# MLA's rotary scores: the two mixed products of a head as one matmul over both halves of the partitions

## The chip, the cores and the metric

The kernel runs on one core of one Trainium2 chip. The metric is device time in microseconds (us); the figure for a kernel is the median of several runs. All times below are in us unless marked otherwise. PE is the matrix engine (TensorE), DVE the vector engine, ACT the scalar engine, POOL GpSimd, and SP issues most of the transfers. PSUM is the memory that PE writes its results to; SBUF is the working memory that all engines read.

## The reference, cut to what matters

One encoder layer on 256 tokens of width 2048: a mixing block (MLA and differential attention side by side, one input projection, one output projection), cross-attention into 256 memory tokens, a SwiGLU feed-forward of 5632, and a final norm. All in float32. The change is in the MLA scores:

```python
s = (jnp.einsum('bqhd,bkhd->bhqk', qn_b, k_nope)      # 8 heads, d = 128
     + jnp.einsum('bqhr,bkr->bhqk', qr_b, k_rope))    # r = 64, one rotary key for all heads
p = jax.nn.softmax(s.astype(jnp.float32) * scale, axis=-1).astype(v.dtype)
```

`q_rope` has 64 numbers for each of 8 heads and passes through a rotation by position; `k_rope` has 64 numbers and is shared by all heads.

## The kernel before, in words

Each float32 operand of a matmul is held as a pair: a high part `h`, the value rounded to fp32r by ACT, and a low part `l`, the rest, subtracted by DVE (`split_into`, L99 and L100). `mm` (L91 to L93) then makes a product in three passes: h·h, h·l and l·h.

Each weight piece arrives in a raw tile (`wraw`, 3 buffers), is split into `wh` (ACT, L99) and `wl` (DVE, L100), 1024 numbers a partition at a time (4 buffers each), and is multiplied into an accumulator in PSUM (`acc`, pool `pacc`, 4 tiles). A second pool in PSUM, `pps`, has 4 tiles of 128x512 and serves everything else on the way: transposes (`pt`), the results of `stationary` (`qT`, `kT`), scores (`psc`), transposed probabilities (`ppt`), products with the values (`po`). A PSUM tile becomes free when its last reader on ACT or DVE is done.

The MLA part runs so. The latents are normalized and transposed into `cqT` and `ckvT` (the latter shares a tile, `lat`, with the rotary keys `krT`). A projection makes the rotary queries `qr`, which DVE rotates. Then for each group `hg` of four heads come queries `qT` and keys `kT` (`stationary`, PE passes of 256 columns) and values `vv` (`values`, an accumulator split into `val_h` and `val_l`). In the first group the rotary queries are transposed in between: 8 transposes into two `pt` tiles, each read by one ACT cast (`qrT_h`) and one DVE subtraction (`qrT_l`). Two heads share a 128-partition block of `qrT`, 64 partitions each; the keys `krT[:, 0]` and `krT[:, 1]` hold the 64 rotary numbers on the one or the other half with zeros on the rest, so that a matmul over 128 partitions picks one head.

The scores of a head and of 128 queries (`scores`) are six passes of 256 columns: three for the 128 plain dimensions and three for the rotary ones. The softmax is a chain over the engines: DVE takes the maximum (`nm`, L432) and scales it (L433), ACT takes the exponentials (`e`, L437), DVE the reciprocal (`rs`, L440) and the scaling (L459), PE transposes (`ppt`, L448), ACT and DVE split the result into `pT_h` and `pT_l`, and PE multiplies with the values (`po`).

What runs beside this on PE are the projections of differential attention (`acc<-wh,x0T`: 128x512, weights `in_w_in`), which need nothing from MLA but accumulators and the weight splits. The order on each engine is not written by hand: the tile framework's scheduler works it out when the program is built, from its own estimates, and it chooses which PSUM slot a new tile takes. On the chip each engine takes its instructions in that fixed order and waits on semaphores; an instruction that waits holds everything behind it on its engine.

## Time and profile before

| | |
|---|---|
| median of 3 runs | 1160.01 (1159.96 to 1160.74) |
| profiled execution | 1160.6, of which the span from first to last instruction is 1158.8 |
| granted PE clock, mean | 0.998 |
| PE busy | 1149.4 of 1158.8 |
| DVE busy | 900.3 |
| ACT busy | 612.1 |
| transfers | 222.13 MB, mean 192 GB/s |

A row of the timeline has the start of an instruction, how long it was busy, its engine, its source line, operation, and what it wrote from what; `x2` means that two equal ones are merged into a row. The busy times of successive instructions overlap a little, so the step from one start to the next (the pitch) is what a queue of them costs.

### The profile page before, as it was taken

The page shows a single profiled execution, that of the slowest core. Times are in us where ns is not written, and L with a number is a line of the kernel's source. Part 1 is how long each engine was busy: PE and PEld are TensorE (multiplying, and loading weights), DVE is VectorE, ACT ScalarE, POOL GpSimd, SP SyncE. Part 2 cuts the span into 40 slices and gives each one's busy share as a digit, 9 for nine tenths or more (in the row PEclk, how much of TensorE's full clock was granted, in tenths as well). Part 3 has the DMA queues.
Part 4 walks back from the last instruction along what each step waited for, and adds up shares of the span by engine and source line. Part 5 has one row for each costly group of instructions (what it writes and reads, how often), then busy time and mean ns, then how long its engine had stood idle before and what let it go on. Part 6 is the DMA issues. An engine that isn't in the chain of part 4 may idle for free.

```text
span 1158.8 us, 14403 instructions
## 1 busy us (share of the span) xinstructions
PE 1149.4 (99%) x5512; PEld 961.6 (83%) x5512; DVE 900.3 (78%) x1192; ACT 612.1 (53%) x866; POOL 69.8 (6%) x81
## 2 busy tenths in 40 slices
PE   9999999999999999999999999999999999999997
PEld 7888888888888888888888888888888888888887
DVE  7588766586867776978888787797888788798873
ACT  6755454554665565655444554564544554554552
POOL 4920000001000000000000000000000000000021
PEclk9999999999999999999999999999999999999999
DMA  9665334445754445465555555655556555565551
GB/s 349 222 205 189 125 137 166 170 146 201 279 210 182 145 147 185 177 218 183 184 213 185 205 185 191 218 180 184 200 186 217 205 181 203 188 220 207 211 198 73
DMA packets 33620, 222.13 MB, mean 192 GB/s; under 512 B 4112, under 2 KB 4752, under 8 KB 8848
## 3 DMA queue, kind: packets, MB, share of 16 engines
q1 hardware_dynamic: 32400, 217.29, 52.4%
q0 software_dynamic: 864, 3.15, 0.8%
q8 instruction: 43, 0.70, 0.2%
q10 hardware_dynamic: 288, 0.79, 0.2%
q14 instruction: 25, 0.20, 0.0%
HBM read 219.11 MB, written 2.10 MB: 191 GB/s over the span
## 4 chain that ended last, share of the span: by engine, by line
PE 98%; issue 0%; DMA 0%; DVE 0%; ACT 0%; SPq 0%; POOLq 0%; POOL 0%; DVEq 0%; ACTq 0%
PE acc L91 28%; PE acc L92 28%; PE acc L93 28%; PE q L91 2%; PE q L92 2%; PE q L93 2%; PE pt L301 2%; PE ppt L448 1%; PE psc L93 1%; PE psc L92 1%; PE psc L91 1%; PE acckv L91 0%; PE acckv L93 0%; PE acckv L92 0%; PE pt L824 0%
## 5 line engine op out<-in xcount | busy, mean ns | idle before, releaser
L99 ACT CAST wh<-wraw 128x1024 fp32r<-128x1024 f32 (+2 forms) x398 | 399.4, 1015 | 386.6 <-PE acc L93 344.4
L100 DVE TENSOR_TENSOR wl<-wraw,wh 128x1024 fp32r<-128x1024 f32 (+2 forms) x398 | 468.4, 1185 | 165.9 <-ACT wh L99 163.9
L92 PE MATMUL acc<-wl,x2n_h 128*128 128x512 f32 x480 | 185.5, 390 | 0.0
L93 PE MATMUL acc<-wh,x2n_l 128*128 128x512 f32 x480 | 185.3, 389 | 0.0
L91 PE MATMUL acc<-wh,x2n_h 128*128 128x512 f32 x480 | 160.5, 390 | 0.0
L93 PEld LDWEIGHTS acc<-wh,x2n_l 128*128 128x128 f32 x480 | 90.1, 188 | 19.0
L91 PEld LDWEIGHTS acc<-wh,x2n_h 128*128 128x128 f32 x480 | 90.1, 188 | 19.0 <-issue 0.2
L92 PEld LDWEIGHTS acc<-wl,x2n_h 128*128 128x128 f32 x480 | 90.1, 188 | 18.7
L92 PE MATMUL acc<-wl,hT_h 128*128 128x512 f32 (+1 forms) x272 | 103.7, 381 | 0.0
L93 PE MATMUL acc<-wh,hT_l 128*128 128x512 f32 (+1 forms) x272 | 103.5, 380 | 0.0
L91 PE MATMUL acc<-wh,hT_h 128*128 128x512 f32 (+1 forms) x272 | 89.4, 382 | 0.0
L92 PE MATMUL acc<-wl,x0T_h 128*128 128x512 f32 x224 | 88.2, 394 | 0.1
L93 PE MATMUL acc<-wh,x0T_l 128*128 128x512 f32 x224 | 87.9, 393 | 0.0
L91 PE MATMUL acc<-wh,x0T_h 128*128 128x512 f32 x224 | 87.7, 396 | 0.0
L99 ACT CAST wh<-tsum 128x1024 fp32r<-128x1024 f32 x56 | 58.3, 1048 | 42.5 <-DVE tsum L698 31.1
L100 DVE TENSOR_TENSOR wl<-tsum,wh 128x1024 fp32r<-128x1024 f32 x56 | 67.9, 1218 | 9.3 <-ACT wh L99 9.3
L91 PEld LDWEIGHTS acc<-wh,hT_h 128*128 128x128 f32 x272 | 51.2, 188 | 9.9 <-issue 0.2
L93 PEld LDWEIGHTS acc<-wh,hT_l 128*128 128x128 f32 x272 | 51.2, 188 | 9.6
L92 PEld LDWEIGHTS acc<-wl,hT_h 128*128 128x128 f32 x272 | 51.2, 188 | 9.5
L91 PEld LDWEIGHTS acc<-wh,x0T_h 128*128 128x128 f32 x224 | 42.3, 189 | 9.0 <-ACT wh L99 1.1
L92 PEld LDWEIGHTS acc<-wl,x0T_h 128*128 128x128 f32 x224 | 42.2, 188 | 8.3 <-DVE wl L100 0.8
L93 PEld LDWEIGHTS acc<-wh,x0T_l 128*128 128x128 f32 x224 | 42.2, 188 | 7.4
(361 smaller groups left out, 2008.4 us busy)
## 6 DMA issues: line engine op xcount, KB each, us to landing
wraw<-in_w_gu SPq DMA_DIRECT2D x80, 1024.0 KB, 4.8
wraw<-in_w_dn SPq DMA_DIRECT2D x36, 1024.0 KB, 4.8
wraw<-in_w_in SPq DMA_DIRECT2D x24, 1024.0 KB, 4.8
wraw<-in_w_out SPq DMA_DIRECT2D x16, 1024.0 KB, 4.9
wraw<-in_w_down SPq DMA_DIRECT2D x8, 1024.0 KB, 4.8
wraw<-in_w_in_lat SPq DMA_DIRECT2D x7, 832.0 KB, 7.2
wraw<-in_w_xk SPq DMA_DIRECT2D x4, 1024.0 KB, 5.8
wraw<-in_w_xq SPq DMA_DIRECT2D x4, 1024.0 KB, 4.8
```

What stands on the lines that cost most here:

```text
L91: nc.tensor.matmul(o, l.h, r.h, start=start, stop=False)
L92: nc.tensor.matmul(o, l.h, r.l, start=False, stop=False)
L93: nc.tensor.matmul(o, l.l, r.h, start=False, stop=stop)
L99: last_cast[0] = nc.scalar.copy(out=dst.h, in_=src).ins
L100: last_split[0] = nc.vector.tensor_tensor(out=dst.l, in0=src, in1=dst.h.bitcast(F32), op=ALU.subtract).ins
L301: nc.tensor.transpose(out=pt[:, j * P:(j + 1) * P], in_=src[:, j * P:(j + 1) * P], identity=ident)
L448: nc.tensor.transpose(out=pt[:, kt * S + tt * P:kt * S + (tt + 1) * P], in_=p[:, tt, kt * P:(kt + 1) * P], identity=ident)
```

## The change

`krT` and the rotary queries are laid out anew. `krT.h` stays. In the half of the partitions where `krT.h[:, o]` has the keys' high part, `krT.l[:, o]` now has a second copy of it, and in the other half the low part. The queries get three tiles instead of two: `qr_h` (the high parts, as before) and `qr_x0`, `qr_x1`, one for each parity of the head, with the low part of the own head on its half and the value again, rounded to fp32r, on the other half. One matmul of `qr_x[o]` with `krT.l[:, o]` then adds up l·h on one half of the partitions and h·l on the other, so a head and 128 queries take five passes instead of six.

```diff
+    def rope_keys(kr, tt):
+        pt = ps_tile("pt")
+        for j in range(2):
+            nc.tensor.transpose(out=pt[:, j * P:(j + 1) * P], in_=kr[:, j * P:(j + 1) * P], identity=ident)
+        pv = pt[:, :2 * P].rearrange("p (j t) -> p j t", t=P)
+        tok = slice(tt * P, (tt + 1) * P)
+        nc.scalar.copy(out=krT.h[:, :, tok], in_=pv)
+        for o in range(2):
+            own = slice(o * 64, o * 64 + 64)
+            nc.scalar.copy(out=krT.l[own, o, tok], in_=pv[own, o])
+            nc.vector.tensor_tensor(out=krT.l[own, 1 - o, tok], in0=pv[own, o],
+                                    in1=krT.h[own, o, tok].bitcast(F32), op=ALU.subtract)
...
-            transposed(krT, kr, tt, 2)
+            rope_keys(kr, tt)
...
-    qrT = act_tile(name="qrT")
+    qr_h = act.tile([P, 4, S], F32R, name="qr_h", tag="act")
+    qr_x = [act.tile([P, 4, S], F32R, name=f"qr_x{o}", tag="act") for o in range(2)]
...
+    def rope_queries(src, tt):
+        pt = ps_tile("pt")
+        for j in range(4):
+            nc.tensor.transpose(out=pt[:, j * P:(j + 1) * P], in_=src[:, j * P:(j + 1) * P], identity=ident)
+        pv = pt.rearrange("p (j t) -> p j t", t=P)
+        tok = slice(tt * P, (tt + 1) * P)
+        nc.scalar.copy(out=qr_h[:, :, tok], in_=pv)
+        for o in range(2):
+            own, other = slice(o * 64, o * 64 + 64), slice((1 - o) * 64, (1 - o) * 64 + 64)
+            nc.vector.tensor_tensor(out=qr_x[o][own, :, tok], in0=pv[own], in1=qr_h[own, :, tok].bitcast(F32),
+                                    op=ALU.subtract)
+            nc.scalar.copy(out=qr_x[o][other, :, tok], in_=pv[own])
...
-                transposed(qrT, qrs[tt], tt, 4)
+                rope_queries(qrs[tt], tt)
...
-    def scores(qs, ks):
+    def scores(q, k, rope=()):
...
-            for n, (q, k) in enumerate(zip(qs, ks)):
-                mm(ps[:, tt * S:(tt + 1) * S], q[:, tt * P:(tt + 1) * P], k, n == 0, n == len(qs) - 1)
+            mm(o, q[:, tok], k, True, not rope)
+            for n, (l, r) in enumerate(rope):
+                nc.tensor.matmul(o, l[:, tok], r, start=False, stop=n == len(rope) - 1)
...
-            ps = [scores([qT[hg][:, h, :], qrT[:, 2 * hg + hp, :]], [kT[hg][:, h, :], krT[:, h % 2, :]])
+            ps = [scores(qT[hg][:, h, :], kT[hg][:, h, :],
+                         [(qr_h[:, 2 * hg + hp, :], krT.h[:, h % 2, :]),
+                          (qr_x[h % 2][:, 2 * hg + hp, :], krT.l[:, h % 2, :])])
```

The other calls of `scores` only change their form. The scheduler lays the program out anew. From a point in the second projection of differential attention on, the rest of PE's, DVE's and ACT's lists is the same in both programs (4580 matmuls and transposes on PE), and POOL's and SP's lists are the same throughout. Between the rotary keys and that point three places differ most.

DVE, around the rotary queries, before (a row has line, operation, what it writes from what, and the engines or transfer queues whose semaphores it waits for):

```order
L100 TENSOR_TENSOR wl<-wraw,wh 128x1024 [waits DMAHW5_49,Activation_49]
L100 TENSOR_TENSOR qrT_l<-pt,qrT_h 128x4x128 [waits Activation_49] x2
L491 SCALAR_TENSOR_TENSOR neg_lam<-lexp 128x1 [waits Activation_49]
L100 TENSOR_TENSOR kT_l<-kT,kT_h 128x512 [waits Activation_49]
L100 TENSOR_TENSOR val_l<-acc,val_h 128x512 [waits Activation_49] x2
L100 TENSOR_TENSOR wl<-wraw,wh 128x1024 [waits DMAHW6_49,PE_49,Activation_49]
```

and in the changed program:

```order
L100 TENSOR_TENSOR wl<-wraw,wh 128x1024 [waits DMAHW5_49,Activation_49]
L437 TENSOR_TENSOR qr_x_770<-pt,qr_h 64x4x128 [waits Activation_49] x2
L526 SCALAR_TENSOR_TENSOR neg_lam<-lexp 128x1 [waits Activation_49]
L100 TENSOR_TENSOR wl<-wraw,wh 128x1024 [waits DMAHW6_49,PE_49,Activation_49]
L437 TENSOR_TENSOR qr_x_771<-pt,qr_h 64x4x128 [waits Activation_49] x2
L100 TENSOR_TENSOR kT_l<-kT,kT_h 128x512 [waits Activation_49] x2
```

The subtractions for `kT_l` have moved behind a weight split and behind two more subtractions.

ACT at the same place, before:

```order
L99 CAST qrT_h<-pt 128x4x128 [waits PE_49] x2
L489 ACT_TABLE_LOAD
L489 ACTIVATE lexp<-ldot 128x2 [waits DVE_49]
L99 CAST kT_h<-kT 128x512 [waits PE_49]
L99 CAST val_h<-acc 128x512 x2
L99 CAST wh<-wraw 128x1024 [waits DMAHW6_49,PE_49]
```

and in the changed program:

```order
L434 CAST qr_h<-pt 128x4x128 [waits PE_49] x2
L524 ACT_TABLE_LOAD
L524 ACTIVATE lexp<-ldot 128x2 [waits DVE_49]
L99 CAST wh<-wraw 128x1024 [waits DMAHW6_49,PE_49]
L439 CAST qr_x_770<-pt 64x4x128 [waits DVE_49] x2
L99 CAST kT_h<-kT 128x512
L99 CAST kT_h<-kT 128x512 [waits PE_49]
L99 CAST val_h<-acc 128x512 x2
L439 CAST qr_x_771<-pt 64x4x128 [waits DVE_49] x2
```

The cast of the weights of the second group's values now stands ahead of everything that empties PSUM. By the values of the semaphores, the copies into `qr_x` (770 is `qr_x0`, 771 `qr_x1`) wait for the subtraction from the same `pt`, and that of `qr_x1` for the copy into `qr_x0`, so a `pt` tile has five readers in turn. On PE the first matmul of the second group's `qT` waited, before, for the first `qrT_l` (it takes over that `pt`'s slot); in the changed program it waits for the first `kT_l` (it takes over the slot of that `kT`).

PE, from the last scores of the first two heads on, before:

```order
L92 MATMUL psc<-lat_l,qrT_h 128x256
L93 MATMUL psc<-lat_h,qrT_l 128x256
L91 MATMUL acc<-wh,x0T_h 128x512 [waits DVE_49]
L92 MATMUL acc<-wl,x0T_h 128x512
L93 MATMUL acc<-wh,x0T_l 128x512
```

and in the changed program:

```order
L459 MATMUL psc<-lat_h,qr_h 128x256
L459 MATMUL psc<-lat_l,qr_x_771 128x256
L481 MATMUL ppt<-ident,e 128x128 [waits DVE_49,PE_49]
L481 MATMUL ppt<-ident,e 128x128 [waits DVE_49]
L481 MATMUL ppt<-ident,e 128x128 x2
```

Before, 57 matmuls of the projection stand between these scores and the first transpose of their probabilities; in the changed program none does. They follow after the first two `po` and the scores of the next two heads. In that stretch ACT and DVE put a split of weights (`wh` on ACT ahead of the exponentials, `wl` on DVE between L465, the maximum, and L466, its scaling).

## The prediction

> **What bounds the kernel now.** I read the page first: span, engines, and the chain of work that ended last.

> ```profile
> span 1158.8 us, 14403 instructions
> ...
> PE 1149.4 (99%) x5512; PEld 961.6 (83%) x5512; DVE 900.3 (78%) x1192; ACT 612.1 (53%) x866; POOL 69.8 (6%) x81
> ...
> PE 98%; issue 0%; DMA 0%; DVE 0%; ACT 0%; SPq 0%; POOLq 0%; POOL 0%; DVEq 0%; ACTq 0%
> ```

> PE is busy for 1149.4 of 1158.8 us, and 98% of the chain lies on PE. So a matmul taken out of PE's list is worth its pitch, and a wait of PE costs its full length, wherever it lies. The profiled execution took 1160.6, which is its span and 1.8 around it; it lies 0.6 above the median 1160.0. I sum differences and put them on the median. About 0.2% (2.3 us) is what a measurement of this kernel can tell from no change.

> Next, the stretch that the change touches, as a table by stages (columns: window, its length, then busy time and count of PE, weight loads, DVE, ACT, POOL; granted clock; share of the DMA engines; GB/s):

> ```profile
> 80.00:90.00 10.00, 10.00 (x80) 9.71 (x79) 9.18 (x14) 7.47 (x13) 1.56 (x2) 1.00 0.75 257
> 90.00:100.00 10.00, 10.00 (x72) 9.42 (x71) 8.65 (x15) 6.62 (x9) 0.00 (x0) 1.00 0.58 205
> ```

> PE has no gap in either window, at full clock. DVE is busy for 9.18 of 10 in the first: there is little room for more work there, and what is put ahead of something urgent delays it.

> **What is taken away.** The rotary passes of the scores, by tile (min/median/max ns, then first and last start):

> ```profile
> L91 PE MATMUL psc<-lat_h,qrT_h x16: 277/283/288, 96.8 to 152.2; 128*128 128x256 f32 x16
> L92 PE MATMUL psc<-lat_l,qrT_h x16: 278/283/283, 97.0 to 152.3; 128*128 128x256 f32 x16
> L93 PE MATMUL psc<-lat_h,qrT_l x16: 280/283/283, 97.1 to 152.4; 128*128 128x256 f32 x16
> ```

> The third row goes: 16 matmuls of 128x256. A busy time of 283 ns is not the price, since successive matmuls overlap. The price is the pitch, and that stands in PE's timeline:

> ```profile
> 81.36 1.04 PE L301 MATMUL pt<-ident,qr 128*128 128x128 f32 x8
> ...
> 82.16 0.36 PE L91 MATMUL kT<-lat_h,wh 128*128 128x256 f32 x1
> ...
> 84.98 0.28 PE L93 MATMUL kT<-lat_h,wl 128*128 128x256 f32 x1
> ...
> 85.11 0.28 PE L91 MATMUL qT<-cqT_h,wh 128*128 128x256 f32 x1
> ...
> 93.75 0.40 PE L91 MATMUL acc<-wh,lat_h 128*128 128x512 f32 x1
> ...
> 96.49 0.28 PE L91 MATMUL psc<-kT_h,qT_h 128*128 128x256 f32 x1
> ...
> 99.36 0.40 PE L91 MATMUL acc<-wh,x0T_h 128*128 128x512 f32 x1
> ```

> From 96.49 to 99.36 lie 24 score matmuls: 2.87/24 = 0.12 each. 16 x 0.12 = 1.9 us off PE. That is the whole gain; the 16 weight loads run beside matmuls. Even untouched by anything else it is 0.16%, inside what counts as the same.

> **What is added.** Four ACT copies and two more DVE subtractions for the queries, and four copies and two more (but smaller) subtractions for the keys. The forms with 64 partitions are not in the trace. Nearest are the rows of as many numbers per partition, and I take their times: a copy at a pitch of 0.48 (two in 1.07, the second busy for 0.59), a subtraction at 0.60. The rows for this:

> ```profile
> 77.14 1.28 DVE L295 TENSOR_TENSOR qr<-qr,ropetmp 128x512 f32<-128x512 f32 x2
> ...
> 82.51 1.07 ACT L99 CAST qrT_h<-pt 128x512 fp32r<-128x512 f32 x2
> ...
> 83.59 1.28 ACT L489 ACT_TABLE_LOAD   x1
> ...
> 86.42 1.07 ACT L99 CAST wh<-wraw 128x1024 fp32r<-128x1024 f32 x1
> ...
> 87.37 0.61 ACT L99 CAST kT_h<-kT 128x512 fp32r<-128x512 f32 x1
> ...
> 84.21 1.28 DVE L100 TENSOR_TENSOR qrT_l<-pt,qrT_h 128x512 fp32r<-128x512 f32 x2
> ...
> 87.52 1.23 DVE L100 TENSOR_TENSOR wl<-wraw,wh 128x1024 fp32r<-128x1024 f32 x1
> ...
> 88.66 0.68 DVE L100 TENSOR_TENSOR kT_l<-kT,kT_h 128x512 fp32r<-128x512 f32 x1
> ...
> 89.26 0.68 DVE L100 TENSOR_TENSOR qT_l<-qT,qT_h 128x512 fp32r<-128x512 f32 x1
> ```

> For the keys, whose pieces are shorter, even four subtractions at 0.60 are 2.4 us on DVE; `qr` is ready at 77.14 + 1.28 = 78.42 and PE transposes it at 81.36, 2.9 later, so this stays covered and costs nothing. If that cover were gone, PE would wait at those transposes. A third tile of 4x256 for the queries comes from a pool of 24 in SBUF; no transfer moves, as the lists of SP and POOL are the same in both programs.

> **The first wait: 4.3 us.** The `pt` tiles now have five readers in turn, so both stay occupied, and with two `kT` tiles all four slots of `pps` are taken. The second group's `qT` (85.11) needs one. Before, it took over the slot of a `pt` whose last reader was `qrT_l`, at 84.21, in time. Now it takes that of the first `kT`, and its last reader, `kT_l`, stands far back. Step by step, on the clock of the rows above:
> - ACT is through the table load at 84.87. Next in its list is the cast of the second group's value weights. It needs the buffer that the first group's `kT` matmuls read until 84.98 + 0.28 = 85.26. It runs for 1.07, to 86.33.
> - DVE does the two subtractions of `qr_x0` where `qrT_l` stood, and then waits for that cast: its `wl` starts at 86.33. The pitch of one is 88.66 - 87.52 = 1.14, so the next starts at 87.47.
> - Two subtractions of `qr_x1`, at 0.60 (89.26 - 88.66): 87.47 and 88.07. Then `kT_l` from 88.67, busy for 0.68, to 89.35. (The ACT copies that these wait for start at 86.21 and 86.69, `kT_h` at 87.17: all earlier.)
> - PE goes on at 89.4 in place of 85.11: 4.3 us. All behind it on PE, and what ACT and DVE do with its results, is late by as much.

> If half the partitions cost half the time, the nearest row is a scaling of 256 numbers, two in 0.62 (a pitch of about 0.27, below): the wait is then 0.7 shorter, 3.6. Upward I allow 0.2 for semaphores: 4.5. I stay with 4.3, since these rows scale with the numbers per partition.

> **The second wait: 3.3 us.** In the changed list the transposes `ppt` follow the first scores at once, and the softmax chain lies bare. Its links:

> ```profile
> 100.57 0.68 DVE L432 TENSOR_REDUCE nm<-psc 128x2 f32<-128x512 f32 x1
> ...
> 97.17 1.05 ACT L99 CAST wh<-wraw 128x1024 fp32r<-128x1024 f32 x1
> ...
> 121.72 0.17 DVE L433 TENSOR_SCALAR nm<-nm 128x2 f32<-128x2 f32 x1
> ...
> 105.99 0.46 ACT L437 ACTIVATE e<-psc,nm 128x256 f32<-128x256 f32 x1
> ...
> 106.36 0.19 ACT L437 ACTIVATION_READ_ACCUMULATOR e<-psc,nm 128x1 f32 x1
> ...
> 106.45 0.46 ACT L437 ACTIVATE e<-psc,nm 128x256 f32<-128x256 f32 x1
> ...
> 107.26 0.16 DVE L440 RECIPROCAL rs<-ssum 128x2 f32<-128x2 f32 x1
> ...
> 107.45 0.62 DVE L459 TENSOR_SCALAR e<-e,rs 128x256 f32<-128x256 f32 x2
> ...
> 113.19 1.08 ACT L99 CAST pT_h<-ppt 128x512 fp32r<-128x512 f32 x2 [1.62 <-PE ppt L448]
> ```

> The scores start at 96.49 + 4.3 = 100.8. The first head has 10 matmuls now; the last starts at 101.88 and ends at 102.16. The maximum runs from 102.2, and DVE's next slot is 102.8. There the list has a `wl` (its cast on ACT, 97.17 before, is now at 101.5 and done at 102.5), which takes the pitch of 1.14 to 103.94. Then the scaling of the maximum (0.17) to 104.1, two exponentials at 0.46, the second's sum read 0.56 after its start: 105.2. The reciprocal, 0.19 later the scalings of 0.62: 106.05. Four transposes at 0.10 (eight from 81.36 to 82.16), the last ending at 106.65; the cast `pT_h`, 0.59: 107.25. PE starts `po` at 107.3. Without waits it would have been there at 100.8 + 20 x 0.12 + 8 x 0.10 = 104.0. So 3.3 us. With that `wl` out of the way it would be 2.2; with 0.2 for the second head's half of the chain, 3.5.

> After that I find no further wait. From 107.3 PE has 32 short matmuls, to 111.1; then 40 of the projection, with four splits (48 matmuls' worth) already in their buffers, so 9.1 us at the pitch of 0.228 (12 from 93.75 to 96.49), during which ACT and DVE catch up. The later head pairs have 25 and more of these, at least 5.7 us, ahead of their transposes, against a chain of some 4.

> **The sum.** -1.9 + 4.3 + 3.3 = +5.7: 1160.0 + 5.7 = 1165.7. By the bounds, from -1.9 + 3.6 + 2.2 = +3.9 to -1.9 + 4.5 + 3.5 = +6.1: 1163.9 to 1166.1.

> **Rivals.**

> *The clock falls in the first gap.* The end of the program, where PE stops, and the start, where it warms up:

> ```profile
> 1150.84 0.28 PE L93 MATMUL acc<-w_h,forms_l 128*128 128x256 f32 x1
> ...
> 1153.00:1154.00 1.00, 0.00 (x0) 0.00 (x0) 0.86 (x3) 0.86 (x1) 0.10 (x1) 1.00 0.00 0
> ...
> 1154.00:1155.00 1.00, 0.00 (x0) 0.00 (x0) 0.42 (x1) 0.07 (x1) 0.00 (x0) 0.67 0.59 214
> ...
> 1155.00:1156.00 1.00, 0.00 (x0) 0.00 (x0) 0.00 (x0) 0.00 (x0) 0.00 (x0) 0.50 1.01 401
> ...
> 1.44 4.45 PE L185 MATMUL wps<-warm 128*128 128x512 bf16 x10 [1.44 <-DVE warm L179]
> ```

> The last matmul ends at 1151.12. The clock (third column from the end) is whole in the next windows, 0.67 in that from 1154 and 0.50 after: it halved at about 1154.3, 3.2 us after PE stopped. The first wait leaves PE idle from 85.26 to 89.4, 4.1 us. Getting back has a price at the start: ten matmuls of 512 columns in 4.45 us, 0.44 each against 0.228 later, so nearly half speed for 4.5 us, and 2.2 us lost. That would give 1167.9. For it: 4.1 is over 3.2. Against: one sample of the delay, and its place relative to the gap is unknown; the second gap, broken by transposes, is shorter. [...]

> *Only one wait is real.* A slot comes free earlier than the list says, or the chain is shorter: -1.9 + 3.3 = +1.4 or -1.9 + 4.3 = +2.4, 1161.4 or 1162.4. For it: DVE has idle time elsewhere. Against: each queue takes its list in order.

> *PE doesn't wait, and the change does what it says.* The place is the first `qT` of the second group. If its slot is free by 85.11, and ACT and DVE get through the chain beside the scores, 1158.1 follows, not slower. This decides if `kT_l` is done 4.3 us earlier than I have it. For it: PE had no idle time in the whole stretch before, with the same scheduler. Against: before, DVE was already busy for 9.18 of 10 there, and the weight cast cannot start before 85.26, nor `kT_l` sooner than 3.4 after it by the rows.

> **How the numbers follow.** Both waits at full clock 0.56 (1163.9 to 1166.1); with the clock falling 0.27 (1167 to 1168.6); one wait alone 0.08 (half of it still within 0.2%); no wait 0.07 (1158.1, within 0.2%; a little chance below it); the rest 0.02. The time named is that of the first. The range of 1163.0 to 1168.6 takes in the first two, 0.83. Slower by over 0.2%, that is over 1162.3: 0.56 + 0.27 + 0.04 + 0.02 = 0.89. Within 0.2%: 0.04 + 0.05 = 0.09. Faster: 0.02.

> **What the profile of the changed kernel would show.** The matmuls of the third rotary pass gone, PE's count down by 16 for the scores. In PE's timeline a gap of some 4 us before the second group's `qT`, released by DVE's `kT_l`, and a second, broken one between the first scores and the first `po`, released by DVE's scaling of `e` and ACT's `pT_h`; no gap anywhere else, and from about 165 us on the same program, some 5.7 later. If the clock fell, the matmuls after the first gap show a pitch of 0.24 rather than 0.12. I would be wrong if the copies and subtractions on 64 partitions cost far from what 128 cost, if a wait in the later head pairs joins in, or if the pause is hidden because PE is ahead.

## The result, and the profile after

| | median of the runs | lowest to highest | runs |
|---|---|---|---|
| before | 1160.26 | 1159.79 to 1161.55 | 6 |
| changed | 1169.97 | 1168.23 to 1170.53 | 6 |

The changed kernel takes 1.0082 times as long (95% interval 1.0071 to 1.0092): 9.7 us slower. Forecast were 5.7, and 1163.0 to 1168.6 as the range. The profiled execution of the changed kernel took 1168.23, with a span of 1166.4; it is the shortest of the six, the other five lie between 1169.64 and 1170.53. So the profile can show one part of the 9.7, and some 2 more remain to be found.

The page of the changed kernel, the lines that answer to those of before:

```profile
span 1166.4 us, 14388 instructions
...
PE 1148.4 (98%) x5496; PEld 961.0 (82%) x5496; DVE 902.2 (77%) x1196; ACT 615.0 (53%) x874; POOL 70.4 (6%) x81
...
PE 97%; DVE 1%; issue 0%; ACT 0%; DMA 0%; SPq 0%; POOLq 0%; POOL 0%; DVEq 0%; ACTq 0%
```

PE has 16 instructions fewer (5496 for 5512), DVE four more and ACT eight more, as the diff says. The span is 7.6 longer, while PE is busy for 1.0 less: its idle time has grown by 8.6. The list of PE's waits between 60 and 180 us (what waits, for whom; sum, times, longest), which was empty before:

```profile
PE qT L91 <- DVE kT_l L100: 4.4, 1, 4.4
PE ppt L481 <- DVE e L492: 2.8, 2, 2.6
```

Both are the waits of the prediction, at their places, and there is no third in this stretch. In PE's timeline:

```profile
85.06 0.28 PE L93 MATMUL kT<-lat_h,wl 128*128 128x256 f32 x1
89.77 0.48 PE L91 MATMUL qT<-cqT_h,wh 128*128 128x256 f32 x1 [4.43 <-DVE kT_l L100]
...
104.99 0.28 PE L459 MATMUL psc<-lat_l,qr_x 128*128 128x256 f32 x1
107.86 0.72 PE L481 MATMUL ppt<-ident,e 128*128 128x128 f32 x4 [2.59 <-DVE e L492]
108.78 0.72 PE L481 MATMUL ppt<-ident,e 128*128 128x128 f32 x4 [0.19 <-DVE e L492]
109.26 0.39 PE L91 MATMUL po<-pT_h,val_h 128*128 128x256 f32 x1
```

A matmul of this kind takes a pitch of 0.12, so PE lost 89.77 - 85.06 - 0.12 = 4.6 at the first wait. From the last score to the first `po` are 109.26 - 104.99 = 4.27; less that score (0.12) and eight transposes at 0.10, the second wait cost 3.35.

Then the clock. The windows here are cut at the moments at which it changes (columns: window, its length, PE's busy time and count, granted clock, share of the DMA engines, GB/s):

```profile
86.43:89.84 3.41, 0.07 (x1) 1.00 0.95 358
89.84:93.25 3.41, 3.41 (x16) 0.50 0.54 223
93.25:96.66 3.41, 3.41 (x30) 1.00 0.02 5
```

Just as PE starts again its clock falls to one half, for 3.41 us. The pitch is 0.21 there in place of 0.12. From the start of `qT` to the last of the first scores (89.77 to 104.99) PE takes 15.2; in e4 and e7 below, where the same 104 matmuls run at full clock, it takes 13.7 to 13.8: 1.5 us lost. Together: -1.9 + 4.6 + 3.35 + 1.5 = 7.55, where the spans differ by 7.6. The profiled execution is explained; the other five lost about two more. The mean clock measured in them is 0.993 or 0.994, against 0.996 in this one; e2's profile below has 0.994, with the clock halved for three such windows in place of one.

### The profile page after: what moved, and what is told of

Same layout as the page of the kernel before. It is cut to its first block, busy times and chain, and to the rows that moved or that the text cites. A ratio compares the mean times of both kernels' runs of the same rounds, so it can differ in the third digit from the quotient of the medians.

```text
span 1166.4 us, 14388 instructions
## 1 busy us (share of the span) xinstructions
PE 1148.4 (98%) x5496; PEld 961.0 (82%) x5496; DVE 902.2 (77%) x1196; ACT 615.0 (53%) x874; POOL 70.4 (6%) x81
## 4 chain that ended last, share of the span: by engine, by line
PE 97%; DVE 1%; issue 0%; ACT 0%; DMA 0%; SPq 0%; POOLq 0%; POOL 0%; DVEq 0%; ACTq 0%
PE acc L91 28%; PE acc L92 28%; PE acc L93 27%; PE q L91 2%; PE q L92 2%; PE q L93 2%; PE pt L301 2%; PE ppt L481 1%; PE acckv L91 0%; PE acckv L93 0%; PE acckv L92 0%; PE qT L91 0%; PE psc L93 0%; PE psc L92 0%; PE psc L91 0%
## 5 line engine op out<-in xcount | busy, mean ns | idle before, releaser
L99 ACT CAST wh<-wraw 128x1024 fp32r<-128x1024 f32 (+2 forms) x398 | 399.1, 1015 | 390.7 <-PE acc L93 351.0
L100 DVE TENSOR_TENSOR wl<-wraw,wh 128x1024 fp32r<-128x1024 f32 (+2 forms) x398 | 466.8, 1181 | 170.5 <-ACT wh L99 168.9
L92 PE MATMUL acc<-wl,x2n_h 128*128 128x512 f32 x480 | 185.4, 390 | 0.0
L93 PE MATMUL acc<-wh,x2n_l 128*128 128x512 f32 x480 | 185.3, 389 | 0.0
L91 PE MATMUL acc<-wh,x2n_h 128*128 128x512 f32 x480 | 160.4, 390 | 0.0
L93 PEld LDWEIGHTS acc<-wh,x2n_l 128*128 128x128 f32 x480 | 90.1, 188 | 19.0
L92 PEld LDWEIGHTS acc<-wl,x2n_h 128*128 128x128 f32 x480 | 90.1, 188 | 18.7
L91 PEld LDWEIGHTS acc<-wh,x2n_h 128*128 128x128 f32 x480 | 90.1, 188 | 18.7
L92 PE MATMUL acc<-wl,hT_h 128*128 128x512 f32 (+1 forms) x272 | 103.7, 381 | 0.0
L93 PE MATMUL acc<-wh,hT_l 128*128 128x512 f32 (+1 forms) x272 | 103.5, 380 | 0.0
L91 PE MATMUL acc<-wh,hT_h 128*128 128x512 f32 (+1 forms) x272 | 89.4, 382 | 0.0
L91 PE MATMUL acc<-wh,x0T_h 128*128 128x512 f32 x224 | 87.0, 393 | 1.4 <-ACT wh L99 1.4
L93 PE MATMUL acc<-wh,x0T_l 128*128 128x512 f32 x224 | 88.2, 394 | 0.0
L92 PE MATMUL acc<-wl,x0T_h 128*128 128x512 f32 x224 | 88.0, 393 | 0.1
L99 ACT CAST wh<-tsum 128x1024 fp32r<-128x1024 f32 x56 | 58.3, 1048 | 42.7 <-DVE tsum L733 31.3
L100 DVE TENSOR_TENSOR wl<-tsum,wh 128x1024 fp32r<-128x1024 f32 x56 | 67.9, 1218 | 9.3 <-ACT wh L99 9.1
L91 PEld LDWEIGHTS acc<-wh,hT_h 128*128 128x128 f32 x272 | 51.2, 188 | 9.9 <-issue 0.2
L93 PEld LDWEIGHTS acc<-wh,hT_l 128*128 128x128 f32 x272 | 51.2, 188 | 9.6
L92 PEld LDWEIGHTS acc<-wl,hT_h 128*128 128x128 f32 x272 | 51.2, 188 | 9.4
L91 PEld LDWEIGHTS acc<-wh,x0T_h 128*128 128x128 f32 x224 | 42.1, 188 | 9.6 <-ACT wh L99 1.9
L92 PEld LDWEIGHTS acc<-wl,x0T_h 128*128 128x128 f32 x224 | 42.1, 188 | 8.8 <-DVE wl L100 1.0
L93 PEld LDWEIGHTS acc<-wh,x0T_l 128*128 128x128 f32 x224 | 42.1, 188 | 7.4
```

Of the source, the lines that this page charges most:

```text
L91: nc.tensor.matmul(o, l.h, r.h, start=start, stop=False)
L92: nc.tensor.matmul(o, l.h, r.l, start=False, stop=False)
L93: nc.tensor.matmul(o, l.l, r.h, start=False, stop=stop)
L99: last_cast[0] = nc.scalar.copy(out=dst.h, in_=src).ins
L100: last_split[0] = nc.vector.tensor_tensor(out=dst.l, in0=src, in1=dst.h.bitcast(F32), op=ALU.subtract).ins
```

## The experiments

All runs beside the kernel before on the same chip; its median was 1160.1 to 1160.3 in each set. "Over before" is the difference of the medians.

| run | median | lowest to highest | over before | what PE waits for in this stage |
|---|---|---|---|---|
| e1 five passes, old layout | 1158.16 | 1157.73 to 1158.86 | -2.1 | nothing |
| e2 mixed matmul twice | 1171.88 | 1171.49 to 1172.24 | +11.6 | 4.4 and 2.3; 0.3, new |
| e3 copy of the queries first | 1164.64 | 1163.64 to 1166.05 | +4.4 | 3.7 at `ppt` |
| e4 half of the copies later | 1164.44 | 1163.08 to 1165.77 | +4.2 | 1.3 and 2.8 |
| e5 both waits gone, projection ahead | 1163.26 | 1161.69 to 1164.87 | +3.2 | 2.4 and 0.7, new |
| e6 second wait gone, projection ahead | 1166.9 | 1165.2 to 1170.06 | +6.8 | 3.3 (for `qr_x`); 2.4 and 0.7, new |
| e7 first wait filled | 1167.69 | 1166.17 to 1168.16 | +7.6 | 1.6 behind the filling, 2.8 |
| e8 changed kernel again | 1169.14 | 1167.42 to 1169.8 | +9.1 | 4.4 and 2.6 |
| e9 e5 with copies of the projection | 1167.01 | 1166.45 to 1168.66 | +6.9 | 3.8, 1.6 and 0.3, new |
| e10 before, in the order of e9 | 1169.26 | 1169.18 to 1169.99 | +9.2 | 4.3 and 2.4, new |
| e11 half of the projection ahead | 1158.69 | 1158.28 to 1159.86 | -1.6 | nothing |
| e12 a quarter of it ahead | 1158.58 | 1157.98 to 1159.89 | -1.7 | nothing |
| e13 first wait alone | 1163.39 | 1161.65 to 1164.97 | +3.2 | 3.3 (for `qr_x`) |
| e14 first wait filled, no second | 1161.2 | 1161.02 to 1161.42 | +1.0 | nothing |
| e15 before, in the order of e11 | 1159.96 | 1159.7 to 1161.26 | -0.2 | nothing |

**The two halves of the change apart (e1, e2).** e1 is the kernel before with the three passes of `mm` written out for the rotary scores, less the one of the queries' low part:

```diff
-                mm(ps[:, tt * S:(tt + 1) * S], q[:, tt * P:(tt + 1) * P], k, n == 0, n == len(qs) - 1)
+                o, l = ps[:, tt * S:(tt + 1) * S], q[:, tt * P:(tt + 1) * P]
+                if n == 0:
+                    mm(o, l, k, True, len(qs) == 1)
+                else:
+                    nc.tensor.matmul(o, l.h, k.h, start=False, stop=False)
+                    nc.tensor.matmul(o, l.h, k.l, start=False, stop=True)
```

> The kernel before with the pass of the rotary scores that multiplies the low part of the queries with the high part of the keys left out (5 passes for a tile instead of 6; the layout, the tiles and the order are those of before). Theory of the prediction: 16 matmuls at 0.12 us go, nothing waits, so -1.9 us: 1158.3. Rival (the passes are not on the path, or something else of the kernel takes the time back): 1160.2, no change.

e2 is the changed kernel with a line more:

```diff
                          [(qr_h[:, 2 * hg + hp, :], krT.h[:, h % 2, :]),
+                          (qr_x[h % 2][:, 2 * hg + hp, :], krT.l[:, h % 2, :]),
                           (qr_x[h % 2][:, 2 * hg + hp, :], krT.l[:, h % 2, :])])
```

> The changed kernel with the mixed matmul of each rotary score issued twice (6 passes as before, the product counted double; the layout and the order of the changed kernel). Theory: only the layout costs, the 16 matmuls give +1.9 us over the changed kernel: about 1171.9 against 1170.0, and both waits of TensorE (4.6 us at the second group's qT, 3.3 us behind the first scores) stand in the profile. Rival (the saved passes are what starves TensorE behind the scores, since they were its cover): the second wait shrinks by the time that the added matmuls run in it, and the time stays near 1170.

e1 gains 2.1 (ratio 0.9979, interval 0.997 to 0.9989), e2 costs 1.9 over the first set of the changed kernel (2.7 over the second, e8). So the saved passes are worth their 1.9 at the pitch of 0.12, which e1 shows best, and the layout alone costs some 11.6. The rival of e2, that the missing passes were the cover, holds for 0.24: the first transposes start 2.63 behind the last score, 2.87 before, since two of the added passes run there. e2's profile also shows a second fall of the clock, on windows of the same length (columns as above):

```profile
84.40:87.81 3.41, 0.54 (x5) 1.00 1.02 420
87.81:91.22 3.41, 1.85 (x9) 0.50 0.99 368
91.22:94.64 3.42, 3.42 (x18) 0.50 0.03 12
...
104.88:108.29 3.41, 1.28 (x11) 1.00 0.24 38
108.29:111.70 3.41, 3.19 (x14) 0.50 0.65 269
```

The clock fell at 87.81, was halved for two windows, and fell again at 108.29: 20.48 later, which is six times 3.413. This is the grid that e8 was to confirm or not.

**The first wait taken away or shortened (e3, e4).** In e3 only the copy `f` holds the PSUM slot:

```diff
-        pv = pt.rearrange("p (j t) -> p j t", t=P)
+        f = nat("qrf")
+        nc.scalar.copy(out=f, in_=pt)
+        pv = f.rearrange("p (j t) -> p j t", t=P)
```

> The changed kernel, with ScalarE copying the transposed queries from PSUM to SBUF first and the five readers of rope_queries reading that copy: the PSUM slot comes free after one copy. Theory (the first wait is the slot, and the clock falls because of that wait): the wait of 4.6 us falls under 1.2, the granted clock stays full, the second wait of 3.3 stays: 1160.3 - 1.9 + 3.3 and up to 1 for the added copies, 1161.7 to 1162.7. Rival A (TensorE waits for the same vector operations at another place, since they are still to be done): 1165 or more, with a new wait in the list. Rival B (the clock falls with the second wait alone): 1163.2 or more.

In e4 the loop over `o` is cut in two (`rope_mixed`), and its second half is written behind the first group's `kT`:

```diff
...
-                rope_queries(qrs[tt], tt)
+                qrs[tt] = rope_queries(qrs[tt], tt)
+                rope_mixed(*qrs[tt], 0)
         kT.append(stationary(weights(a["w_ukv_k"][hg]), ckvT, 2, "kT"))
+        if hg == 0:
+            for tt in range(NT):
+                rope_mixed(*qrs[tt], 1)
```

> The changed kernel, with the second half (o = 1) of what rope_queries makes traced behind the keys of the first group: the vector copy that frees the slot stands one 64-partition operation earlier in its queue. Theory (the wait is as long as the queue ahead of that copy): 4.6 - 1.3 = 3.3 us, the second wait 3.3. If the clock falls after a gap of a length between 3.3 and 4.6, it stays full here: 1160.3 - 1.9 + 3.3 + 3.3 = 1165.0. Rival (the clock falls after any such gap): 1166.5 to 1168.5.

In e3 PE runs from `kT` into `qT` with no wait: the slot was the cause. But the median is 2 to 3 above the theory's, since rivals A and B both held in part. PE comes to the scores 4.6 earlier, and DVE is not ready by as much. PE's wait, and then DVE's list there:

```profile
PE ppt L483 <- DVE e L494: 3.7, 1, 3.7
```

```profile
97.90 0.68 DVE L467 TENSOR_REDUCE nm<-psc 128x2 f32<-128x512 f32 x1
98.50 1.21 DVE L100 TENSOR_TENSOR wl<-wraw,wh 128x1024 fp32r<-128x1024 f32 x1
99.63 0.68 DVE L467 TENSOR_REDUCE nm<-psc 128x2 f32<-128x512 f32 x1
100.23 0.28 DVE L468 TENSOR_SCALAR nm<-nm 128x2 f32<-128x2 f32 x2
```

A weight split and the second head's maximum stand between the first head's maximum and its scaling. From the last score at 98.29 to `po` at 103.98 it is 5.69, less 0.92 of work: 4.8 in place of 3.35. With -1.9 that is +2.9. The clock adds to it: it is halved from 102.3 to 105.7 in the profile (part of the transposes is in the 4.8 already), so here the second wait, listed with 3.7, made it fall alone. Behind `po` that costs 0.75 more there; this run is the fastest of the five, at +3.4, and the rest of the median's +4.4 is not shown.

e4 came out near the theory's time (1164.44 for 1165.0), but by luck, with other terms. Its waits:

```profile
PE ppt L488 <- DVE e L499: 2.8, 2, 2.6
PE qT L91 <- DVE kT_l L100: 1.3, 1, 1.3
```

The first is 1.3 in place of 3.3, and behind it the clock stayed full (1.00 from 84 to 105.5). -1.9 + 1.4 + 3.35 make +2.9; the clock, which the theory had full, fell behind the second wait. From the last of the first scores on, the list is 1.5 later than in the changed kernel's profile, where the clock stayed full there; that is the rest of the +4.2.

**Filling and repeating (e7, e8).** e7 has PE work in the first wait, and changes nothing else (`zero` is a tile of zeros):

```diff
...
+            if fill and hp == 1:
+                for n in range(fill):
+                    nc.tensor.matmul(ps[:, S:2 * S], zero, xT[:, 0, :].h, start=False, stop=n == fill - 1)
             split_into(t[:, 2 * hp:2 * hp + 2, :], ps.rearrange("p (j t) -> p j t", j=2))
...
-        kT.append(stationary(weights(a["w_ukv_k"][hg]), ckvT, 2, "kT"))
+        kT.append(stationary(weights(a["w_ukv_k"][hg]), ckvT, 2, "kT", 24 if hg == 0 else 0))
```

> The changed kernel with 24 matmuls that add zero, each 0.12 us, at the end of the second key tile of the first group: TensorE works through 2.9 of the 4.6 us for which it waited, and the second group's qT starts no earlier. Theory (in the median run the halved clock costs more than in the profiled one, since both waits can halve it): the first wait no longer halves it, 1170.0 - 2 to 3.5, so 1166.5 to 1168. Rival (the clock's fall is a small part, and the spread of the times has another cause): 1169.5 or more; a slot that comes free later for it would show as a longer wait behind the added matmuls.

> The changed kernel itself, for a second profile of it. Theory (the clock is judged in stretches of 3.4 us on a grid of their own, 89.84 and 93.25 us in the first profile, so that each run meets the two waits at another phase): a profile near 1170 shows the clock halved for two stretches behind the first wait, or halved a second time behind the second, and the lost clock makes up the difference from 1168.2. Rival: the halved stretch is the one of 3.4 us as before and the difference lies in a wait that is longer.

In e7 `qT` starts 4.6 after the last real `kT` matmul, as in the changed kernel, and the clock stays full there (1.00 from 83.9 to 94.2); the median is 1.45 below that of e8, inside the theory's range. By the waits and the passes alone e7 would be at 1160.1 + 6.05 = 1166.1. Of the 1.55 above that its profile shows 1.5 behind the second wait, where the clock is halved from 108.0 to 111.4: by so much the same matmuls are later there than in the changed kernel's profile.

e8's profiled run took 1169.15, and shows what the first profile lacked:

```profile
86.97:90.38 3.41, 0.84 (x7) 1.00 1.00 377
90.38:93.79 3.41, 3.41 (x18) 0.50 0.33 137
...
104.04:107.45 3.41, 1.00 (x9) 1.00 0.32 43
107.45:110.86 3.41, 3.23 (x15) 0.50 0.63 264
```

The clock fell twice, at 90.38 and at 107.45, 17.07 apart, five times 3.41. The waits are as long as before. The first fall cost 1.5 again (15.22 from `qT` to the last of the first scores), the second 1.0, by which the list behind it is later than in the first profile: -1.9 + 4.6 + 3.35 + 1.5 + 1.0 = 8.55, where the spans differ by 8.5. So the theory held, and the rival did not: at waits as long as before, a second halved stretch makes up the difference, with falls at 90.38 and 107.45 where the first profile has one, at 89.84. In the ten profiles in which the clock fell between 80 and 140 us (the changed kernel, e2 to e5, e7 to e10, e13) it stayed halved for 3.41 each time, or for two times that (6.83), and in the changed kernel's profile its changes at 89.84, 93.25 and 1161.62 follow each other by 1 and by 313 times 3.413. That a run's loss hangs on where its two waits lie on this grid is the author's reading of these profiles, not shown by itself.

**The second wait taken away (e5, e6, e9, e10).** e5 has the copy of e3, and this (`first` is set for the second group's values):

```diff
...
-            split_into(t[:, tt, :n], accs[tt][:, :n], None if r is None else r[:, tt:tt + 1])
+            src = accs[tt]
+            if first:
+                src = nat("vf")
+                nc.scalar.copy(out=src, in_=accs[tt])
+            split_into(t[:, tt, :n], src[:, :n], None if r is None else r[:, tt:tt + 1])
...
+    acc_dk = diff_project(0, 1)
     mixT = []
...
-    dk0 = diff_rope(diff_project(0, 1))
+    dk0 = diff_rope(acc_dk)
```

> The kernel of e3 (ScalarE copies the transposed queries to SBUF first), and beside it ScalarE copies the second group's value sums to SBUF ahead of their split, and the differential branch's key projection is written ahead of the heads, so that its matmuls stand behind the first scores. Theory (the two waits and the clock that falls with them are all that the change costs): TensorE runs through, the clock stays full, 1160.3 - 1.9 = 1158.4. Rival (the layout has another cost, or the wait moves on to a later place): 1160.5 or more, with a new wait in the list.

e6 is e5 with the copies of `rope_queries` reading PSUM:

```diff
-        f = nat("qrf")
-        nc.scalar.copy(out=f, in_=pt)
-        pv = f.rearrange("p (j t) -> p j t", t=P)
+        pv = pt.rearrange("p (j t) -> p j t", t=P)
```

> The changed kernel with only the second half of that edit: ScalarE's copy of the second group's value sums, and the key projection ahead of the heads; the copies of rope_queries still read PSUM. Theory: the first wait stays near 4 us and halves the clock for 1.5 to 2.6 us more, the second is gone: 1160.3 - 1.9 + 4 + 2 = 1164.4 (1163.5 to 1165.5). Rival (each wait alone takes what both take together, since one bound stands behind both): near 1168 or more.

Both rivals came true in part. The two waits of PE were gone in e5 (in e6 the second), and two others had come, the same in both:

```profile
PE acc L91 <- DVE dn L293: 2.4, 1, 2.4
PE po L91 <- ACT pT_h L99: 0.7, 1, 0.7
```

With the whole projection ahead of the heads, its accumulators are held until DVE has rotated the keys, and that stands behind the softmax chains. -1.9 + 2.4 + 0.7 = +1.2; e5's fastest run has +1.6, the median +3.2, with the clock halved behind the new wait in the profile (130.27 to 133.68). e6 lies between its theory (1164.4) and its rival (1168). Its first wait is now for the last reader of a `pt` tile, the same in e13 further down:

```profile
PE qT L91 <- ACT qr_x L443: 3.3, 1, 3.3
```

Its profiled run, 1165.69, has the clock full behind all its waits (1.00 from 82 to 170), its slowest, 1170.06, a mean clock of 0.993. e9 has copies of those accumulators as well, and e10 is the kernel before with the order of e9:

```diff
-    acc_dk = diff_project(0, 1)
+    acc_dk = []
+    for acc in diff_project(0, 1):
+        acc_dk.append(nat("dkf"))
+        nc.scalar.copy(out=acc_dk[-1], in_=acc)
```

> The kernel of e5, and ScalarE also copies the two halves of the differential branch's key projection to SBUF as they end, so that the accumulators for its value projection come free without the rotation on VectorE (the new wait of e5, 2.4 us at the acc behind dn). Theory (e5 lost only by that wait, the 0.7 us at po and the clock that fell behind them): 1160.1 - 1.9 + up to 0.7 = 1158.2 to 1158.9, the clock full. Rival (VectorE is behind in this whole stage, so that TensorE waits for it at whatever place comes first): 1160.5 or more with another wait in the list.

> The kernel before with the same order and the copies of the value sums and of the key projection on ScalarE (the rotary layout as before, six passes). Theory: it had no wait of TensorE in this stage, so nothing is to be gained: 1160.1, within 0.5. Rival (the reordering itself gives or costs time, and so the time of e9 is not the passes'): off by more than 1 us.

Both theories fell. e9's waits first, then e10's:

```profile
PE acc L92 <- DVE wl L100: 3.8, 1, 3.8
PE acc L91 <- ACT wh L99: 1.6, 1, 1.6
```

```profile
PE acc L91 <- ACT wh L99: 4.3, 1, 4.3
PE acc L92 <- DVE wl L100: 2.4, 1, 2.4
```

The whole projection at one go uses up the weight splits that are ready, and the next ones stand behind the heads' work on ACT and DVE. That order costs the kernel before even more (9.2) than the changed one (6.9). So e9 tells of the order, not of the layout. That this holds for e5 and e6 too is likely but not shown, since no run has their order in the kernel before. A better place for the projection was wanted.

**The projection in two parts (e11, e12, e15).** e11 is e3 with the copy of the value sums, and with the heads (the loop over `hg`, as a function `mla_heads`) written between the second and third of the four pieces of the key projection's weights: `project` calls `before(i)` ahead of piece `i`. In e12 it is `i == 1`; e15 is the kernel before with the copy of the value sums and the order of e11. The line of e11, against e5:

```diff
-    acc_dk = diff_project(0, 1)
+    acc_dk = project(x0T, [w_in[2, i] for i in range(4)], before=lambda i: i == 2 and mla_heads())
```

> The kernel of e3 with ScalarE's copy of the second group's value sums (as in e5), but of the key projection only the first two of its four weight pieces are written ahead of the heads: 44 of its matmuls (5.3 us) stand between the first scores and the first transposes, and the other 48 come in among the heads, where the kernel before has them. Theory (the two waits and the clock are all that the change costs, and e5, e9 and e10 lost by the projection's place, not by the layout): no wait of TensorE over 1 us in this stage, the clock full, 1160.1 - 1.9 = 1158.2, up to 1159.2. Rival (VectorE and ScalarE are short of time in this stage, so that a wait comes up at a later place): 1161 or more.

> As e11, with only the first of the four pieces ahead: some 20 matmuls behind the first scores, 2.4 us, against a softmax chain that was bare for 4.6 us in e3. Theory: a wait of about 1 to 2 us is left at the transposes, too short for the clock: 1159.2 to 1160.4. Rival: as for e11, 1161 or more.

> The kernel before with the order and the copy of value sums of e11 (six passes, the rotary layout as before). Theory (the order gives nothing where TensorE had no wait; what e11 gained is the passes): 1160.2, within 0.5. Rival (part of the gain of e11 is the order's): 1159.3 or less.

e11 takes 0.9987 of the time before (interval 0.9978 to 0.9996), e12 0.9985 (0.9976 to 0.9994): 1.6 and 1.7 faster, what the passes are worth. Both beat both kernels, if by less than the 0.2% named in the prediction. e12 did better than its theory: no wait was left. The theory had 20 matmuls of 0.12 as cover; in the profile 35 of the projection's, at a pitch of 0.23, stand between the first scores and the transposes, 8 us. Its windows, with all engines (PE, weight loads, DVE, ACT, POOL, clock, DMA, GB/s):

```profile
80.00:90.00 10.00, 10.00 (x83) 9.80 (x82) 8.53 (x12) 8.98 (x16) 0.00 (x0) 1.00 0.60 211
90.00:100.00 10.00, 10.00 (x68) 9.21 (x67) 9.51 (x14) 7.59 (x12) 0.09 (x1) 1.00 0.69 249
100.00:110.00 10.00, 10.00 (x50) 8.34 (x49) 7.22 (x15) 7.22 (x15) 1.47 (x2) 1.00 0.52 175
```

PE is busy throughout, at full clock, though DVE and ACT do all the work that the layout adds, and more copies. e15 is level with before (0.9999, 0.999 to 1.0007), so the order by itself gives nothing, and the gain is that of the passes.

**The clock's price behind the first wait (e13, e14).** e13 is e11 with the copies of `rope_queries` reading PSUM (the diff of e6); e14 is e13 with the filling of e7.

> The kernel of e11 without ScalarE's copy of the transposed queries: rope_queries reads PSUM again, so the first wait is back (3.3 to 4.6 us, as in e6), and the second is not. Theory: where the clock stays full 1160.2 - 1.9 + 3.3 to 4.6 = 1161.6 to 1162.9; it falls in some executions and not in others, by how the wait lies on the grid of 3.4 us, and adds 1.7 to 2.6 there: times spread over more than 2 us, median 1162.5 to 1164.5. Rival (the spread comes from the second wait or from something else): the times agree within 1 us.

> The kernel of e13 with the 24 matmuls of e7 that add zero, 2.9 us of work in that wait. Theory: qT starts no earlier, the clock never falls, so the times lie at the lower end of those of e13 and agree within 1 us: 1161.6 to 1162.9. The difference of the two medians is what the clock costs behind the first wait alone. Rival (the clock has nothing to do with the spread): the same median and spread as e13.

e13 spreads over 3.3 us, e14 over 0.4; not all of the 3.3 is the wait's, as e1, e11, e12 and e15, where nothing waits, spread over 1.1 to 1.9. e14's `qT` comes right behind the filling, 3.0 after the last real `kT`, against 3.5 in e13, so 0.5 of the 2.2 between the medians is the wait's, and 1.7 the clock's. By its wait e14 should take 1160.2 - 1.9 + 3.0 = 1161.3 at full clock, and it takes 1161.2. By its wait e13 should take 1160.2 - 1.9 + 3.5 = 1161.8 without a fall; its fastest run has 1161.65, at a mean clock of 0.998. Its median is 1.7 above that, its slowest 3.3. The profiled one has this:

```profile
84.61:88.02 3.41, 0.74 (x7) 1.00 0.99 336
88.02:91.43 3.41, 2.75 (x13) 0.50 0.98 396
91.43:94.85 3.42, 3.42 (x18) 0.50 0.22 89
94.85:98.26 3.41, 3.41 (x30) 1.00 0.00 0
```

PE starts again at 88.68; busy for 2.75 of the first halved window, it stays halved for a second. From the start of `qT` to the last of the first scores it takes 16.45, and e14 13.76 for the same matmuls: 2.7 lost.

## Why the prediction was wrong, point by point

- **What goes (-1.9).** Right: -2.1 in e1, +1.9 in e2.
- **What 64 partitions cost.** Right: two `qr_x` copies of 64x512 take 1.06 on ACT, two subtractions 1.27 to 1.30 on DVE, as much as on 128 (1.07 and 1.28 in the kernel before). The keys' part is covered: PE waits nowhere between 10 and 85 us.
- **The first wait (4.3).** Right in place, cause and size (4.6). The links on DVE, and the cast on ACT for which `wl` waits, in order of time:

```profile
84.43 1.27 DVE L437 TENSOR_TENSOR qr_x<-pt,qr_h 64x512 fp32r<-64x512 f32 x2
...
85.26 1.04 ACT L99 CAST wh<-wraw 128x1024 fp32r<-128x1024 f32 x1
...
86.34 1.23 DVE L100 TENSOR_TENSOR wl<-wraw,wh 128x1024 fp32r<-128x1024 f32 x1 [0.57 <-ACT wh L99]
87.59 1.30 DVE L437 TENSOR_TENSOR qr_x<-pt,qr_h 64x512 fp32r<-64x512 f32 x2
88.93 1.29 DVE L100 TENSOR_TENSOR kT_l<-kT,kT_h 128x512 fp32r<-128x512 f32 x2
```

  The `wl` started at 86.34 (86.33 forecast). The row of `kT_l` merges two; it starts at 88.93, 0.26 later than forecast, and PE follows 0.84 behind (0.7 forecast). With 4.6 it lies 0.1 above the upper bound, in which 0.2 for semaphores was the author's estimate.
- **The second wait (3.3).** Right: 3.35. The weight split lies in the chain as described:

```profile
104.11 0.69 DVE L465 TENSOR_REDUCE nm<-psc 128x2 f32<-128x512 f32 x1 [1.11 <-PE psc L459]
104.72 1.22 DVE L100 TENSOR_TENSOR wl<-wraw,wh 128x1024 fp32r<-128x1024 f32 x1
105.85 0.16 DVE L466 TENSOR_SCALAR nm<-nm 128x2 f32<-128x2 f32 x1
```

- **The sum.** +5.7 at full clock; the same terms as measured make +6.05. This is what the kernel would cost at full clock, and no run had it.
- **The clock: the step that failed.** The prediction made "both waits at full clock" the likeliest, at 0.56, and gave the fall 0.27 and a price of 2.2 (its bound of 1168.6 is 0.3 above its own upper terms, 1166.1 + 2.2). The mean clock of all ten runs (six and four) was 0.993 to 0.996, against 0.997 to 0.999 in e1, e11, e12 and e15, where nothing waits. Two things were wrong. First, the condition: the 0.27 was the author's estimate from one delay, 3.2, against a gap of 4.1, and no run shows that chance; in its place the clock fell in each of the three profiles that have the wait of 4.4 (the changed kernel, e2, e8). Nor did PE have to be idle throughout: the clock fell behind windows in which it was busy for 0.54 (e2), 0.84 (e8) and 1.28 (e2) of 3.41. At the end of the kernel before, too, the last of the work (0.20) lies within the 3.41 ahead of the fall (1150.92 to 1154.34). If windows of 3.41 follow each other, an idle time of 4.4, as the profile counts the first wait, leaves one with at least 2.2 of it, so at most 1.2 busy; the fall came behind 0.07 (the changed kernel), 0.54 (e2) and 0.84 (e8). Second, the place: the second wait was called shorter and broken, and no fall was priced there. It fell there in the profiles of e2, e3, e4, e7 and e8. The first fall's price was put somewhat high (1.5 for one halved window, 2.7 for two in e13; a pitch of 0.21, not 0.24); the second's, 1.0 in e8 and 1.5 in e4 and e7, was missing. The profiled e8, at +9.1, is explained by its terms (8.55, with the spans 8.5 apart; the profiled run of the kernel before lies 0.5 above its median). The 9.7 of the first set is 0.6 more than e8's median, and its five slower runs have no profile. An estimate for them, not shown: with two halved windows behind the first wait, as in e13, and one behind the second, as in e8, -1.9 + 4.6 + 3.35 + 2.7 + 1.0 = 9.75.
- **How the clock came back.** The prediction had it come back after 4.5 us, from the start of the program. In the profiles it was full again behind halved windows in which PE was busy for 3.19 (e2), 3.23 (e8) and 3.41 (the changed kernel) of 3.41, and stayed halved for another behind windows with 1.85 (e2) and 2.75 (e13).
- **What stays open** is where the bound for a fall lies. With the ten profiles cut at whole numbers of 3.413 from a fall, the clock fell behind each of the 11 full-clock windows between 80 and 140 us in which PE was busy for up to 1.53 (e4). Behind those from 1.56 (e8) up it stayed full, with one exception: it fell behind 104.55 to 107.97 in e7 (1.80, mostly transposes), and not behind 103.49 to 106.90 in the changed kernel (1.78, no transposes). How transposes count is not settled: 106.90 to 110.32 in the changed kernel, with eight of them in its 2.26, stayed full.

## What to carry to other kernels

A wait of the engine that bounds the kernel had two prices here: its length, and the clock that fell behind it (4.6 and 1.5 at the first wait of the changed kernel's profile). The wait that is listed with 4.4 brought the fall in all three profiles that have it, and waits listed with 2.4 to 3.3 in some and not in others. A spread between equal runs was a hint of it (3.3 in e13), and filling the wait with work that adds nothing told what it costs (1.7 of the 2.2 between the medians of e13 and e14). When a saving lengthens the lists of other engines, look at what holds the buffers, and at what was standing beside the chain that is now bare: here copies of two kinds of tile and another place for a quarter of a projection (e12) turned +9.7 into -1.7.

## What the runs showed of the hardware that was not expected

```profile
83.51:86.92 3.41, 1.64 (x14) 1.00 0.95 380
86.92:90.34 3.42, 1.87 (x15) 1.00 0.93 357
```

In one profile the fall came late, when PE was already back at work. In e4 the transposes start at 104.0 and `po` at 105.4, and the clock falls at 105.73, which the rows miss by 0.04:

```profile
102.36:105.77 3.41, 1.57 (x11) 0.99 0.64 240
105.77:109.18 3.41, 3.41 (x19) 0.51 0.16 67
```
